# A hybrid decoder step on one core: order from changed prices, weights stored tile by tile, and two rows turned by TensorE

## The chip, the core and the metric

The kernel runs on one core of one Trainium2 chip. The core has five engines that run side by side, each with its own queue of instructions that it works off strictly in order: TensorE (PE in the profile, its weight loads PEld), VectorE (DVE), ScalarE (ACT), GpSimd (POOL) and SyncE (SP), which here only issues DMAs. The metric is the device time of one execution in microseconds (us). An instruction that waits for another engine holds up everything behind it in its own queue, so the order in each queue matters as much as the amount of work.

## The reference

One layer of a decoder for 1024 prompt tokens and 8 single-token samples, all in 32-bit floats, model width 1024:

```python
p = x @ w_in                                    # 1024 x 9360
p_gla, p_rwkv, p_gate = split(p)
# branch 1, gated linear attention, 4 heads, in chunks
#   S_t = diag(a_t) S_{t-1} + k_t^T v_t ;  o_t = q_t S_t
# branch 2, RWKV-7, 16 heads of 64, after a shift by one token
#   S_t = S_{t-1} (diag(w_t) - kk_t^T (kk_t * a_t)) + v_t^T k_t ;  y_t = S_t r_t
m = (sigmoid(gate_a) * (o_gla @ w_up_gla)
     + sigmoid(gate_b) * (o_rwkv @ w_up_rwkv))
y = layernorm(2**0.25 * x + m @ w_out)
```

Each branch norms its output and multiplies it with a gate. The final states of both branches and the last row of the shift are outputs too.

## The kernel before

The tokens are worked in two passes: pass 0 has 512 prompt tokens and the 8 samples (two tiles of 260 columns), pass 1 the other 512 prompt tokens (one tile of 512). Activations lie transposed, features on the 128 partitions. A product with a weight is made in blocks of 128 output features. Weight and input are each split into a high and a low part (`wpart`, `xh`, `xl`), and three products (high with high, high with low, low with high) are summed, 24 matmuls for each tile.

**Weights** (`load_w`). Half a block of a weight, 512 x 128 values, is loaded into a buffer `wraw` of 128 partitions x 512 values (three buffers), ACT rounds it to the high part, DVE subtracts to get the low part, and in pass 0 the split weight is stored to DRAM and loaded from there in pass 1 (`w`). In DRAM `w_in` is a matrix with 9360 columns, so each partition of `wraw` gets four runs of 128 values, 512 bytes each.

**RWKV pairs** (`pair`). Two heads make a pair, 8 pairs in each pass, 16 in all. `front` makes decays and products of a pair: it fills `BK` (a `wide` buffer: 8 chunks of 128 x 128 values, the rows called b and k), `az` and `gg`, sends part of `gg` through DRAM (`LD`) into a second `wide` buffer `L`, and solves a triangular system in 31 steps on DVE (`Xt`, `X`, the first step reads `L`). `back` finishes the inverse. `turn` (lines 1185 to 1204) transposes `BK` and the row v: DVE transposes blocks of 32 x 32, and then copies put each block where it belongs, 16 copies for `BK` and 8 for v in each pair, on ACT or DVE. `chain` runs over the 8 chunks of 64 tokens, one after another, each a row of short steps that go back and forth: a matmul into `pch`, a copy to `rh` on DVE, a matmul, two copies to `u` (a `wide` buffer), a matmul, two DVE operations that make the next state (`Sp` after the last chunk). `norm` ends the pair.

**GLA heads** (`gla_head`) use `row` buffers, a state `S` and PSUM banks called `big`; their transposes are done by TensorE with the identity from `cons`.

**The order** (`Order.run`). Nothing here is ordered by hand. Each strand of work is a generator that offers one operation at a time. A planner keeps a model time for every engine and every tile, prices each operation (`price`), finds when it could start (`start`: when its engine is free and its inputs are ready, plus a margin for the way between engines, `HOP`, and 0.4 us more, `SPARE`, where TensorE reads what another engine made), and takes the one with the earliest start, shifted by a priority. Where an operation may run on two engines (`C`: ACT or DVE, `E`: DVE or POOL), the one that would end it first gets it. The list that comes out is the program; on the chip only that order and the waits on semaphores count. Every recorded operation carries the same line in the profile, L215 (the line in the helper), so its groups are told apart by the names of tiles. Projection matmuls (`proj`) are long in supply and are put between the steps of pairs and heads.

Of the kernel before, what the change touches and what calls it, by code (L numbers as in the profile page):

```python
# [20 lines left out]
P = 128  # L21
D = 1024
NK = D // P
# [3 lines left out]
HT = TP // 2  # L27
# [6 lines left out]
NCH = HT // C  # L34
# [3 lines left out]
OFF_Q, OFF_K, OFF_V, OFF_G, OFF_A = 0, 512, 1024, 2048, 3072  # L38
OFF_R = 3088
# [24 lines left out]
HOP = {"P": 0.2, "D": 0.26, "G": 0.14, "V": 0.14, "A": 0.14}  # L64
# [5 lines left out]
AGE = 0.5  # L70

SPARE = 0.4
BIAS = 0.1
ASIDE = 0.5

# [67 lines left out]
def price(eng, name, out, args, ins):  # L143

    n = out.free_size()
    src = [x for x in ins if x.tensor.space != PSUM] if eng == "A" else ins
    if eng == "P":
        m = args[0].free_size()
        rows, cols = tiles(name, args)
        if name == "transpose":  # L150
            return 0.112
        if args[0].dtype == F32R:
            return max(m / 1200, n / 2200) if rows == cols == P else (m + n) / 1200
        if rows == cols == P:
            return 2 * max(m, n) / 1200 + 0.005
        return 2 * (m + n) / 1200 * rows * cols / P ** 2
    if eng == "S":
        return 0.48
    if eng == "A":
        extra = len(ins) - 1  # L160
        return 0.052 + n / 1200 + (0.042 if len(src) == len(ins) else 0.0) + 0.094 * extra
    wide = max([n, *(x.free_size() for x in ins)]) if name in ("tensor_reduce", "bn_stats", "bn_aggr") else n
    if eng == "V":
        if name == "tensor_tensor_scan":
            return 0.1 + n / 480
        if name in ("tensor_copy", "copy", "memset") and ins and ins[0].tensor.space != PSUM:
            wide = wide / 2
        scalars = sum(x.free_size() == 1 for x in ins[1:]) if name in ("scalar_tensor_tensor", "tensor_scalar") else 0
        return 0.068 + wide / 960 + 0.06 * scalars
    if name in ("tensor_scalar", "memset"):  # L170
        return 0.08 + n / 760
    return 0.1 + n / (300 if name == "tensor_copy" else 456)
# [64 lines left out]
class Order:  # L237
# [83 lines left out]
    def start(self, op):  # L321

        best = None
        for eng, fn, cost in op.ways:
            free, t = self.time[eng] + (SWITCH if eng == "P" and op.tiles != self.tiles else 0.0), 0.0
            for x in (op.out, *op.ins):
                at, by = self.ready.get(x.tensor.name, (0.0, None))
                if eng == "S" and by == "D" and x is op.out:
                    continue
                if by != eng:  # L330
                    at += HOP.get(by, 0.0) + (SPARE if eng == "P" and by in ("V", "A", "G") else 0.0)
                elif eng != "P" and x is not op.out:
                    at += 0.13
                t = max(t, at)
            t = max(t, self.read.get(op.out.tensor.name, 0.0))
            if eng in op.port:
                free = max(free, self.port["G" if eng == "V" else "V"])
            late, t = free - t, max(t, free)
            if eng in "VA" and self.held(eng, op):
                cost += HOLD  # L340
            end = t + cost
            if len(op.ways) > 1:
                end += BIAS if eng == "V" and "A" in op.ways[0][0] else ASIDE if eng == "G" and "G" in op.port else 0.0
            if best is None or end < best[0]:
                best = end, t
                op.eng, op.fn, op.cost, op.late = eng, fn, cost, max(0.0, late)
        return best[1]
# [55 lines left out]
class Kern(Order):  # L403
# [219 lines left out]
    def load_w(self):  # L623

        H = NK // 2
        todo = [(b.src, b.c0, j, b.c.i) for b in self.plan if b.src is not None for j in range(2)]
        raws, his, los, kept = [], [], [], {}

        def high():
            n = 0  # L630
            while True:
                yield lambda: len(raws) > n
                w = yield from self.get("wpart")
                yield self.A.copy(w[:, 0], raws[n][0])
                his.append(w)
                n += 1
                if n == count:
                    return

        def low():  # L640
            for n in range(count):
                yield lambda: len(his) > n
                w = his[n]
                raw, src, c0, j, i = raws[n]
                yield self.E.tensor_sub(w[:, 1], raw, w[:, 0].bitcast(F32))
                self.free(raw)
                los.append(w)
                if src is self.a["w_in"] and i == 0:
                    kept[c0, j] = self.dr.tile([P, 2, 512], F32, name=f"w{c0}_{j}")
                    yield self.S.dma_start(kept[c0, j], w.bitcast(F32))  # L650
                self.ws.append(w)
            self.w_done = True
        count = sum(src is not self.a["w_in"] or i == 0 for src, _, _, i in todo)
        self.spawn(high(), "w")
        self.spawn(low(), "w")
        for n, (src, c0, j, i) in enumerate(todo):
            if src is self.a["w_in"] and i:
                yield lambda: len(los) == len(raws)
                w = yield from self.get("wpart")
                yield self.S.dma_start(w.bitcast(F32), kept[c0, j])  # L660
                self.ws.append(w)
                continue
            raw = yield from self.get("wraw")
            op = self.S.dma_start(raw.rearrange("p (k c) -> p k c", c=P),
                                  src[j * H * P:(j + 1) * H * P, c0:c0 + P].rearrange("(k p) c -> p k c", p=P))
            yield from self.load(f"w{n}", op)
            raws.append((raw, src, c0, j, i))

    def blocks(self):
# [515 lines left out]
    def turn(self, d):  # L1185

        q = [slice(32 * n, 32 * n + 32) for n in range(4)]
        t, tv_ = d.L.rearrange("p (c j f) -> p c j f", c=NCH, j=4), (yield from self.row(HT))
        yield self.V.transpose(d.L, d.BK.rearrange("p c t -> p (c t)"))
        yield self.V.transpose(tv_, d.v[:, :HT])  # L1190
        self.free(d.v)
        for i in range(4):
            for j in range(4):
                yield self.C.copy(d.BK[q[j], :, q[i]], t[q[i], :, j])
        self.free(d.L)
        u = yield from self.get("wide")
        d.u = u.rearrange("p (c h v) -> p c h v", c=NCH, h=2)
        tv = tv_.rearrange("p (c j f) -> p c j f", c=NCH, j=2)
        for h in range(2):
            for i in range(2):  # L1200
                for j in range(2):
                    yield self.C.copy(d.u[q[2 - 2 * h + j], :, h, q[i]], tv[q[2 * h + i], :, j])
        self.free(tv_)
# [445 lines left out]
LANE = ["rwkv_w0", "rwkv_a0", "rwkv_k_k", "rwkv_k_a", "rwkv_r_k", "rwkv_lnx_w", "rwkv_lnx_b"]  # L1649


def layout(i):
    f = np.ascontiguousarray
    cst, lev, heads = constants()
    ch = lambda v: v.reshape(-1, P).T
    pv = np.concatenate([ch(i["rwkv_mu"][0]), ch(i["rwkv_w0"][0]), ch(i["rwkv_a0"][0]), ch(i["rwkv_k_k"][0]),
                         ch(i["rwkv_k_a"][0]), ch(i["rwkv_r_k"][0].reshape(-1)), ch(i["rwkv_lnx_w"][0]),
                         ch(i["rwkv_lnx_b"][0]), ch(i["gla_alpha_b"][0]), ch(i["gla_norm_w"][0])], axis=1)
    xp, xs = i["x_prompt"][0], i["x_sample"][:, 0]
    x = np.concatenate([xp, xs], axis=0)  # L1660
    xT = f(np.concatenate([xp[:HT], xs, xp[HT:]], axis=0).T)
    return {
        "cst": cst, "lev": lev, "heads": heads, "pv": f(pv), "xT": xT, "x": f(x), "w_in": f(i["w_in"][0]),
        "wa": f(i["w_in"][0][:, OFF_A:OFF_R].reshape(NK, P, 16).transpose(1, 0, 2).reshape(P, NK * 16)),
        "gla_alpha_w2": f(i["gla_alpha_w2"][0]), "state_gla": f(i["state_gla"]), "state_rwkv": f(i["state_rwkv"]),
        "shiftT": f(i["state_rwkv_shift"][0].reshape(NS, NRC, P).transpose(2, 1, 0)),
        "lora2": f(np.stack([np.concatenate([i[n][0]] * 2, axis=0) for n in ("rwkv_w2", "rwkv_a2")], axis=1)),
        "lane": f(np.concatenate([i[n][0].reshape(RH, RN) for n in LANE], axis=1)),
        "w_up_gla": f(i["w_up_gla"][0]), "w_up_rwkv": f(i["w_up_rwkv"][0]), "w_out": f(i["w_out"][0]),
        "ln": f(np.concatenate([i["ln_g"], i["ln_b"]], axis=0)),  # L1670
    }

# [19 lines left out]
```

## Time and profile before

| what | value |
|---|---|
| median of 3 runs (lowest to highest) | 1630.72 us (1629.09 to 1632.49) |
| the profiled execution, its time | 1630.17 us |
| its span in the profile | 1628.4 us |
| PE busy, matmuls | 1559.5 us, 96% |
| DVE busy | 1304.1 us, 80% |
| ACT busy | 900.1 us, 55% |
| POOL busy | 131.0 us, 8% |
| DMA, share of 16 engines in use | 62.9% |

The profiled execution took 0.55 us less than the median of the runs; 1.77 us of its time lie outside the span. Busy times of PE come from matmuls that overlap: a matmul's own duration is longer than the distance to the next.

### The profile page before, as it was taken

To read this page: it belongs to the slowest core of one execution; us is meant where nothing else is said; L and a number is where in the kernel's file an instruction comes from. 1 tells how busy PE (TensorE), PEld (TensorE's weight loads), DVE (VectorE), ACT (ScalarE), POOL (GpSimd) and SP (SyncE) were. 2 spreads that over 40 slices of the span, in tenths; PEclk is the share of its full clock that TensorE was granted. 3 is DMA by queue.
4 is the path that set the end of the run, shared out by engine and by line. 5 is a ranking of instruction groups with operands and counts; after the bars stand their busy time and mean duration, and the time that the engine had idled before them with its cause. 6 is when DMAs were issued, how large, how long until landed. Compare 5 with 4: busy or idle time off the path is not lost. (4 is left out here: it accounts for less than half of the span.)

```text
span 1628.4 us, 29162 instructions
## 1 busy us (share of the span) xinstructions
PE 1559.5 (96%) x9874; PEld 1375.1 (84%) x9874; DVE 1304.1 (80%) x3407; ACT 900.1 (55%) x2185; POOL 131.0 (8%) x207
## 2 busy tenths in 40 slices
PE   8999999999999998999999999999899999999998
PEld 7999999998989997787877787787778789977786
DVE  6787899888978897797778898989779877656555
ACT  5557676665677666564755463456344757644210
POOL 1010010000110001000101011111111100000000
PEclk9999999999999999999999999999999999999999
DMA  9867876686767774655555446644563687788432
GB/s 293 261 199 235 250 252 187 207 241 224 235 187 225 247 231 133 218 161 153 155 169 170 123 156 197 177 116 152 159 202 111 197 239 240 232 279 266 143 111 84
DMA packets 287281, 318.27 MB, mean 195 GB/s; under 512 B 87203, under 2 KB 210092, under 8 KB 287132
## 3 DMA queue, kind: packets, MB, share of 16 engines
q1 hardware_dynamic: 287132, 316.40, 62.9%
q8 instruction: 79, 1.29, 0.3%
q14 instruction: 70, 0.57, 0.1%
HBM read 196.66 MB, written 118.61 MB: 194 GB/s over the span
## 5 line engine op out<-in xcount | busy, mean ns | idle before, releaser
L215 PE MATMUL proj<-xh,wpart 128*128 128x260 f32 (+1 forms) x3760 | 927.5, 330 | 1.9 <-DMA wpart<-w 1.1
L215 PEld LDWEIGHTS proj<-xh,wpart 128*128 128x128 f32 x3760 | 630.7, 190 | 52.6 <-issue 5.6
L215 PE MATMUL proj<-xl,wpart 128*128 128x260 f32 (+1 forms) x1880 | 615.5, 327 | 0.0
L215 PEld LDWEIGHTS proj<-xl,wpart 128*128 128x128 f32 x1880 | 356.6, 190 | 25.6 <-issue 3.4
L215 ACT CAST wpart<-wraw 128x512 fp32r<-128x512 f32 x210 | 129.5, 621 | 84.3 <-PE proj L215 37.6
L215 DVE TENSOR_TENSOR row<-row 128x512 f32<-128x512 f32 (+9 forms) x314 | 158.1, 508 | 16.9 <-DMA row<-state_rwkv 9.6
L215 DVE TENSOR_TENSOR wpart<-wraw,wpart 128x512 fp32r<-128x512 f32 x202 | 140.4, 702 | 37.4 <-ACT wpart L215 33.9
L215 ACT ACTIVATE row<-row 128x512 f32<-128x512 f32 (+4 forms) x229 | 138.6, 611 | 33.8 <-DVE row L215 19.4
L215 DVE TENSOR_TENSOR Xt<-X,wide 128x60 f32<-128x60 f32 (+24 forms) x496 | 108.6, 219 | 29.3 <-DMA wide<-LD 18.3
L215 PE MATMUL big<-row 128*128 128x64 f32 (+4 forms) x712 | 116.1, 278 | 8.3 <-DVE S L215 4.2
L215 ACT ACTIVATE s0p<-wide,pc 64x64 f32<-64x64 f32 x256 | 88.2, 344 | 53.1 <-DVE wide L215 40.0
L215 DVE TENSOR_TENSOR X<-X,Xt 128x60 f32<-128x60 f32 (+24 forms) x496 | 108.2, 218 | 10.9
L215 PEld LDWEIGHTS big<-row 128*128 128x128 f32 (+1 forms) x712 | 98.2, 191 | 17.5 <-DVE row L215 4.6
L215 POOL TENSOR_TENSOR row<-row 128x512 f32<-128x512 f32 (+7 forms) x55 | 62.3, 1138 | 560.1 <-DVE X L215 160.0
L215 ACT ACTIVATE row<-proj,omu 128x260 f32<-128x260 f32 (+1 forms) x99 | 54.2, 548 | 92.9 <-PE proj L215 92.3
L215 ACT COPY wide<-pch 64x64 f32<-64x64 f32 x226 | 46.7, 207 | 92.3 <-PE pch L215 85.0
L215 DVE SCALAR_TENSOR_TENSOR wide<-pch,pc,s0p 64x64 f32<-64x64 f32 x224 | 63.0, 281 | 32.0 <-PE pch L215 27.6
L215 ACT COPY wide<-wide 32x256 f32<-32x256 f32 x182 | 73.4, 403 | 23.3 <-DVE wide L215 21.2
L215 ACT COPY row<-big 128x128 f32<-128x128 f32 (+7 forms) x174 | 47.3, 296 | 57.5 <-PE big L215 55.4
L215 DVE SCALAR_TENSOR_TENSOR row<-proj,pv,row 128x259 f32<-128x259 f32 (+1 forms) x99 | 56.3, 569 | 23.7 <-ACT tail L215 14.9
L215 PE MATMUL big<-xh,wpart 128*128 128x260 f32 (+1 forms) x288 | 73.1, 332 | 0.7 <-DVE wpart L215 0.2
L215 PE MATMUL big<-az,wide 128*128 128x256 f32 x256 | 67.5, 395 | 3.8 <-ACT row L215 1.6
(243 smaller groups left out, 2540.5 us busy)
## 6 DMA issues: line engine op xcount, KB each, us to landing
w<-wpart SPq DMA_DIRECT2D x146, 512.0 KB
wpart<-w SPq DMA_DIRECT2D x146, 512.0 KB
wraw<-w_in SPq DMA_DIRECT2D x146, 256.0 KB
wide<-LD SPq DMA_DIRECT2D x64, 128.0 KB
wraw<-w_up_gla SPq DMA_DIRECT2D x32, 256.0 KB
wraw<-w_up_rwkv SPq DMA_DIRECT2D x32, 256.0 KB
sg<-row SPq DMA_DIRECT2D x16, 260.0 KB
row<-sg SPq DMA_DIRECT2D x16, 260.0 KB
```

The lines of the kernel that those rows point to most:

```text
L215: ways.append((eng, lambda call=call: call(out, *args, **kw), price(eng, name, out, args, ins)))
```

## The change

Three things change.

1. **Prices and margins of the planner.** A matmul of 32-bit rounded type costs n/2165 us for n columns, in place of n/2200; issuing a DMA 0.56 us, in place of 0.48; any ACT operation 0.045 us more; and whatever reads a tile that a DMA filled is planned 0.5 us later (`LANDED`).
2. **Weights are laid out on the host** as they are loaded (`blocked`): half a block of `w_in`, `w_up_gla` and `w_up_rwkv` is one contiguous piece, 2 KB for each partition. The load is one plain copy. The number of loads and their bytes stay.
3. **`turn`**: `BK` is transposed by TensorE, four 128 x 128 transposes into one `big` bank and one copy of 128 x 512 back, twice for each pair. The row v goes as before. `u` takes the buffer of `L` in place of another `wide` buffer.

```diff
+LANDED = 0.5
...
-            return max(m / 1200, n / 2200) if rows == cols == P else (m + n) / 1200
+            return max(m / 1200, n / 2165) if rows == cols == P else (m + n) / 1200
...
-        return 0.48
+        return 0.56
...
-        return 0.052 + n / 1200 + (0.042 if len(src) == len(ins) else 0.0) + 0.094 * extra
+        return 0.097 + n / 1200 + (0.042 if len(src) == len(ins) else 0.0) + 0.094 * extra
...
-                    at += HOP.get(by, 0.0) + (SPARE if eng == "P" and by in ("V", "A", "G") else 0.0)
+                    at += HOP.get(by, 0.0) + (SPARE if eng == "P" and by in ("V", "A", "G") else LANDED if by == "D" else 0.0)
...
-            op = self.S.dma_start(raw.rearrange("p (k c) -> p k c", c=P),
-                                  src[j * H * P:(j + 1) * H * P, c0:c0 + P].rearrange("(k p) c -> p k c", p=P))
-            yield from self.load(f"w{n}", op)
+            yield from self.load(f"w{n}", self.S.dma_start(raw, src[c0 // P, j]))
...
     def turn(self, d):
         q = [slice(32 * n, 32 * n + 32) for n in range(4)]
-        t, tv_ = d.L.rearrange("p (c j f) -> p c j f", c=NCH, j=4), (yield from self.row(HT))
-        yield self.V.transpose(d.L, d.BK.rearrange("p c t -> p (c t)"))
+        for x in range(0, NCH, 4):
+            pt = yield from self.bank("big", [P, 4, P])
+            for n in range(4):
+                yield self.tr(pt[:, n], d.BK[:, x + n])
+            yield self.C.copy(d.BK[:, x:x + 4], pt)
+            self.free(pt)
+        tv_ = yield from self.row(HT)
         yield self.V.transpose(tv_, d.v[:, :HT])
         self.free(d.v)
-        for i in range(4):
-            for j in range(4):
-                yield self.C.copy(d.BK[q[j], :, q[i]], t[q[i], :, j])
-        self.free(d.L)
-        u = yield from self.get("wide")
-        d.u = u.rearrange("p (c h v) -> p c h v", c=NCH, h=2)
+        d.u = d.L.rearrange("p (c h v) -> p c h v", c=NCH, h=2)
...
+def blocked(w):
+    return np.ascontiguousarray(w.reshape(2, NK // 2, P, -1, P).transpose(3, 0, 2, 1, 4).reshape(-1, 2, P, NK // 2 * P))
```

With new prices the whole list is dealt anew on every engine. Counted over the program, TensorE gets 128 transposes more (`big<-cons,wide`); DVE loses 16 block transposes of 128 x 1024; 256 block copies (182 on ACT, 74 on DVE) give way to 32 copies of 128 x 512 (26 on ACT, 6 on DVE); of the 256 copies from `pch` to `u`, ACT had 226 and now has 120, DVE had 30 and now has 136; ACT loads its function tables 57 times in place of 49.

DVE at the turn of the fourth pair of pass 0, before (`az`, `wide<-row` and `XT` end `front` and `back`, the copies after the two transposes are `turn`; numbers in names are buffers):

```order
L215 TENSOR_TENSOR az_167<-row 64x8x64 x2
L215 COPY pc<-row 128x8
L215 TENSOR_TENSOR wide<-row 64x8x64 x3
L215 COPY XT_172<-big 32x4x32
L215 TENSOR_TENSOR wide<-row 64x8x64
L215 STREAM_TRANSPOSE wide<-wide 128x1024
L215 STREAM_TRANSPOSE row<-row 128x512
L215 COPY wide<-wide 32x8x32 x15
L215 COPY wide<-row 32x8x32 x8
L215 TENSOR_TENSOR wpart<-wraw,wpart 128x512 x3
L215 COPY rh<-pch 128x128
```

and now, from the first of the two big copies on:

```order
L216 COPY wide<-big 128x512
L216 TENSOR_TENSOR az_167<-row 64x8x64
L216 COPY pc<-row 128x8
L216 TENSOR_TENSOR wide<-row 64x8x64
L216 COPY wide<-big 128x512
L216 STREAM_TRANSPOSE row<-row 128x512
L216 TENSOR_TENSOR wide<-row 64x8x64 x3
L216 COPY wide<-row 32x8x32 x3
L216 TENSOR_TENSOR wpart<-wraw,wpart 128x512
L216 SCALAR_TENSOR_TENSOR row<-row,pv 128x512
```

Twenty-three copies in a row stood between the transposes and the next pair's first `rh`; five remain on DVE, with other work between them.

DVE at the start of the triangular solve of the sixth pair of pass 1, before (`Xt<-X,wide` with 31 columns is the first reader of `L`; `Sp<-pch` makes the last state of the pair ahead):

```order
L215 TENSOR_TENSOR Xt<-X,wide 128x31
L215 TENSOR_TENSOR X<-X,Xt 128x31
L215 TENSOR_TENSOR Xt<-X,wide 128x30
L215 TENSOR_TENSOR X<-X,Xt 128x30
L215 TENSOR_TENSOR Xt<-X,wide 128x29
L215 TENSOR_TENSOR X<-X,Xt 128x29
L215 TENSOR_TENSOR Xt<-X,wide 128x28
L215 TENSOR_TENSOR X<-X,Xt 128x28
L215 TENSOR_TENSOR Xt<-X,wide 128x54
L215 TENSOR_TENSOR X<-X,Xt 128x2x27
L215 SCALAR_TENSOR_TENSOR Sp<-pch,pc,s0p 64x64 x2
L215 TENSOR_TENSOR Xt<-X,wide 128x52
```

and now:

```order
L216 SCALAR_TENSOR_TENSOR Sp<-pch,pc,s0p 64x64 x2
L216 TENSOR_TENSOR row<-st,row 128x512
L216 CAST part<-row 128x512
L216 TENSOR_TENSOR row<-row 128x512
L216 TENSOR_TENSOR part<-row,part 128x512
L216 TENSOR_TENSOR row<-row 128x512 x2
L216 SCALAR_TENSOR_TENSOR row<-big,row 128x512
L216 TENSOR_TENSOR row<-row 128x512
L216 TENSOR_REDUCE row<-row 128x8
L216 TENSOR_TENSOR part<-row,part 128x512
L216 TENSOR_TENSOR Xt<-X,wide 128x31
```

The state now stands ahead of the first reader of `L` with ten other operations between them; before, it stood ten operations behind it.

More of the change, by code (lines that the diff above doesn't have):

```diff
@@ L1662, in layout @@
     return {
-        "cst": cst, "lev": lev, "heads": heads, "pv": f(pv), "xT": xT, "x": f(x), "w_in": f(i["w_in"][0]),
+        "cst": cst, "lev": lev, "heads": heads, "pv": f(pv), "xT": xT, "x": f(x), "w_in": f(np.concatenate([blocked(i["w_in"][0][:, :OFF_A]), blocked(i["w_in"][0][:, OFF_R:])])),
         "wa": f(i["w_in"][0][:, OFF_A:OFF_R].reshape(NK, P, 16).transpose(1, 0, 2).reshape(P, NK * 16)),
@@ L1668, in layout @@
         "lane": f(np.concatenate([i[n][0].reshape(RH, RN) for n in LANE], axis=1)),
-        "w_up_gla": f(i["w_up_gla"][0]), "w_up_rwkv": f(i["w_up_rwkv"][0]), "w_out": f(i["w_out"][0]),
+        "w_up_gla": blocked(i["w_up_gla"][0]), "w_up_rwkv": blocked(i["w_up_rwkv"][0]), "w_out": f(i["w_out"][0]),
         "ln": f(np.concatenate([i["ln_g"], i["ln_b"]], axis=0)),
```

## Prediction

> **What bounds the kernel now.** I read the page's sums first, then the stretches, then who waited for whom, TensorE's waits first.
>
> ```profile
> span 1628.4 us, 29162 instructions
> PE 1559.5 (96%) x9874; PEld 1375.1 (84%) x9874; DVE 1304.1 (80%) x3407; ACT 900.1 (55%) x2185; POOL 131.0 (8%) x207
> PEclk9999999999999999999999999999999999999999
> ```
>
> ```profile
> 1446.23:1451.78 5.55, 5.55 (x26) 4.50 (x25) 2.58 (x4) 2.91 (x5) 0.00 (x0) 1.00 0.76 229
> 100.00:1280.00 1180.00, 1131.70 (x7276) 1004.19 (x7275) 1001.26 (x2772) 704.54 (x1777) 114.15 (x176) 0.99 0.61 188
> 1480.00:1628.40 148.40, 140.65 (x629) 113.90 (x629) 84.51 (x133) 26.67 (x53) 2.77 (x3) 0.99 0.42 133
> ```
>
> TensorE bounds: it is idle for 1628.4 - 1559.5 = 68.9 us, at full clock throughout. 48.3 us of the idle time lie in the long middle (1180 - 1131.7), where projections and pairs are mixed; 7.8 us lie in the last stretch, mostly after its last matmul, and nothing of the change reaches those. So the time is TensorE's own work plus its waits, and an edit is worth what it does to either. Its waits:
>
> ```profile
> PE pch L215 <- DVE wide L215: 8.6, 8, 3.7
> PE big L215 <- DMA row<-xT: 8.0, 5, 4.1
> PE big L215 <- DVE S L215: 7.8, 4, 4.2
> PE big L215 <- DVE part L215: 6.2, 6, 1.4
> PE pch L215 <- DVE rh L215: 6.2, 8, 1.7
> PE big L215 <- DVE Sp L215: 5.7, 2, 4.8
> PE big L215 <- DVE row L215: 4.1, 6, 1.3
> PE proj L215 <- DMA wpart<-w: 1.1, 1, 1.1
> PE proj L215 <- DVE wpart L215: 0.7, 2, 0.4
> ```
>
> The six rows of DVE make 38.6 us; the weights (the last two) make 1.8 us. So TensorE is held up by a DVE that is late, and the question is why it is late. Two places show two causes. At 370 us DVE does the copies of a turn without a break, and the first matmul of a chain waits:
>
> ```profile
> 370.62 4.47 DVE L215 COPY wide<-wide 32x256 f32<-32x256 f32 x15
> 375.11 2.37 DVE L215 COPY wide<-row 32x256 f32<-32x256 f32 x8
> 377.63 0.46 PE L215 MATMUL pch<-wide,gg 128*128 128x128 f32 x2 [3.69 <-DVE wide L215]
> ```
>
> At 1149 us DVE itself waits for a DMA, the one that brings `L`; the state of the chain stands behind that in its queue, and TensorE waits for the state:
>
> ```profile
> 1149.21 0.19 DVE L215 TENSOR_TENSOR Xt<-X,wide 128x31 f32<-128x31 f32 x1 [3.33 <-DMA wide<-LD]
> 1153.42 0.59 DVE L215 SCALAR_TENSOR_TENSOR Sp<-pch,pc,s0p 64x64 f32<-64x64 f32 x2
> 1154.07 0.42 PE L215 MATMUL big<-cons,Sp 128*64 128x128 f32 x1 [4.84 <-DVE Sp L215]
> ```
>
> What DVE waits for, over the whole span:
>
> ```profile
> DVE wpart L215 <- ACT wpart L215: 33.9, 34, 3.8
> DVE row L215 <- ACT row L215: 18.3, 15, 2.5
> DVE Xt L215 <- DMA wide<-LD: 18.3, 11, 4.0
> DVE row L215 <- ACT tail L215: 14.9, 24, 2.4
> DVE row L215 <- DMA row<-state_rwkv: 9.6, 4, 3.3
> DVE S L215 <- ACT row L215: 8.5, 9, 2.4
> ```
>
> For DMAs 27.9 us in 15 waits, 1.86 us each; for ACT 75.6 us in 82 waits, 0.92 us each. These are waits the planner did not foresee, or it would have put other work there.
>
> **The change part by part.** Each term is against the span.
>
> ```profile
> L215 ACT COPY wide<-wide 32x256 f32<-32x256 f32 x182 | 73.4, 403 | 23.3 <-DVE wide L215 21.2
> L215 DVE COPY wide<-wide 32x256 f32<-32x256 f32 x74 | 23.1, 312 | 1.2
> L215 DVE STREAM_TRANSPOSE wide<-wide 128x1024 f32<-128x1024 f32 x16 | 19.8, 1239 | 0.1
> L215 ACT ACTIVATE row<-big,pv 128x512 f32<-128x512 f32 x36 | 23.5, 687 | 8.4 <-PE big L215 8.1
> L215 PE MATMUL big<-cons,row 128*128 128x128 f32 x96 | 16.6, 272 | 0.0
> 625.90 0.49 PE L215 MATMUL big<-cons,row 128*128 128x128 f32 x3
> L215 ACT CAST wpart<-wraw 128x512 fp32r<-128x512 f32 x210 | 129.5, 621 | 84.3 <-PE proj L215 37.6 <-PE big L215 18.3 <-issue 7.0
> ```
>
> *Transposes on TensorE: +14.0.* A transpose takes 272 ns, but three in a row take 0.49 us, so the next ends (0.49 - 0.272)/2 = 0.109 us later; 128 of them make 14.0 us. They lie on the engine that bounds, with nothing to hide them. Ends: 14.0, and 34.8 if none overlapped (128 x 0.272). I take the low end, since the three stand in the same mix of matmuls.
>
> [...]
>
> *The turn's copies: -3.7.* ACT loses 73.4 us, DVE 23.1 + 19.8 = 42.9; 32 copies of 128 x 512 out of PSUM come instead, 32 x 0.687 = 22.0 us by the nearest row, most on ACT. Neither engine bounds, so this counts only where TensorE waited: 3.7 us at 370 us, where the order now leaves five copies. Ends 0 and -8.6, the whole row of `pch` waiting for DVE's `wide`; I take the one wait that is seen behind the copies.
>
> *Margin behind DMAs: -8.3.* `L` hangs on two landings in a row (`LD`, then `L`) and eight issues, so its reader is planned 2 x 0.5 + 8 x 0.08 = 1.64 us later, 88% of a mean wait of 1.86. Of the 38.6 - 3.7 = 34.9 us that are left, DMAs have a share of 27.9 / (27.9 + 75.6) = 27%, so 34.9 x 0.27 x 0.88 = 8.3. The order bears this out at 1149 us, where the state now stands ahead of the reader. Ends 0 and -9.4 (the full share).
>
> *ACT's price: -11.5.* A cast of 128 x 512 was priced 0.052 + 512/1200 + 0.042 = 0.521 us and takes 0.621; the new 0.566 closes 45% of the gap. ACT's share of the 34.9 is 73%: 34.9 x 0.73 x 0.45 = 11.5. Ends -25.5 and, if the new deal makes other waits of the same size, 0.
>
> *Weight loads behind waits: -3.1.* The weight load of a matmul waits too, and part of that does not show as an idle PE:
>
> ```profile
> PEld pch L215 <- DVE rh L215: 16.3, 30, 2.1
> ```
>
> 16.3 us there against 6.2 us of PE: 10.1 us in which the next matmul was not ready while the last still ran. Half of it, 5 us, I count as lost; of DVE's waits (3.7 + 8.3 + 11.5)/38.6 = 61% go, so 3.1. Ends 0 and -6.
>
> *New waits: +4.2.* Each of the 32 groups of transposes needs `BK` finished and a free bank out of three, then a copy; and 106 copies to `u`, 53 steps of chains, move from ACT to the fuller DVE.
>
> ```profile
> L215 ACT COPY wide<-pch 64x64 f32<-64x64 f32 x226 | 46.7, 207 | 92.3 <-PE pch L215 85.0 <-DVE wide L215 2.1 <-issue 1.1
> L215 DVE COPY wide<-pch 64x64 f32<-64x64 f32 x30 | 6.6, 219 | 2.6 <-PE pch L215 1.8 <-issue 0.2
> ```
>
> The copy itself takes as long on either (207 and 219 ns). A chain step that DVE serves costs TensorE 6.2/128 = 0.049 us by the row of `rh` (128 steps); (32 + 53) x 0.049 = 4.2. Ends 0 and 22.0, if every group waited for its copy of 0.687.
>
> *Weights as they are loaded: 0.* 210 loads go from 512 packets of 512 B to 128 of 2 KB.
>
> ```profile
> DMA packets 287281, 318.27 MB, mean 195 GB/s; under 512 B 87203, under 2 KB 210092, under 8 KB 287132
> ```
>
> Packets should fall by 210 x 384 = 80,640 to about 206,600. TensorE waited for weights 1.8 us, so the loads are covered by three raw and four split buffers; were that cover gone, ACT and DVE would show it as waits for `wraw`. Ends -1.8 and 0; a larger packet gives no reason for a loss.
>
> Two edits cost nothing. The first is the matmul's price. The chain of work that ended last has a block of 24 matmuls of 512 columns back to back:
>
> ```profile
> 1446.23 5.55 PE proj L215 x24
> ```
>
> That is 0.231 us each; the old price gave 0.233 and the new gives 0.236, 5 ns apart at most from what is measured, against a margin of 400. The second is eight more table loads on ACT, which is idle for 45% of the span:
>
> ```profile
> L382 ACT ACT_TABLE_LOAD x48 | 61.6, 1283 | 0.8
> ```
>
> 8 x 1.28 = 10.3 us, less than the copies ACT sheds. SP issues the same 1299 DMAs, POOL gets six operations more at 8% busy. What comes late next where DVE's waits go is the chain itself: its steps have about 1 us of projections between them either way.
>
> **The sum.** 14.0 - 3.7 - 8.3 - 11.5 - 3.1 + 4.2 = -8.4, a span of 1620.0. With the 1.77 us outside the span this execution would take 1621.8, and 0.55 more for the median: 1622.
>
> **The rivals.**
>
> *The waits are dealt out anew* (slower). Nothing makes DVE faster: it loses 42.9 us and gets 106 copies (23 us) and 6 big ones (4 us). The margin in front of TensorE stays 0.4 us, and an order dealt anew may hit other late landings as often. Then the margin, ACT's price and the weight loads bring 0 and 14.0 - 3.7 + 4.2 = +14.5 remain: 1645. It decides where those three bring less than 14.5 us together, in place of the 22.9 I count, and the loss is clear below 11.2. For it speaks that DVE is 85% busy in the middle (1001.26 of 1180); against it, that two of the three longest waits are seen to go in the order.
>
> *Transposes do not overlap*, if the data come too late for one to follow the other: 34.8 in place of 14.0, 20.8 more: 1643. Against it stands the row of three. [...]
>
> *The planner becomes right* (much faster). Every wait for DVE goes, with the 5 us of weight loads: 14.0 - 38.6 - 5 + 4.2 = -25.4, 1605. [...] The stretch of those 5.55 us (the first of the three above), in which PE never idles, has 4.50 us of weight loads, 81%, so here 84% is no headroom; the gain ends at the waits.
>
> *It cancels*, recovered waits near 14 us with no new ones: 1631.
>
> **How the numbers follow.** A difference under 0.2%, 3.3 us, cannot be told from none. Forecast, 1613 to 1630: 0.40. Much faster: 0.19. Cancels: 0.07. Waits dealt anew: 0.28. No overlap: 0.06. The forecast's upper end (1627.5 on) counts as the same, about 0.02. Faster is 0.38 + 0.19 = 0.57, same 0.09, slower 0.34. The range runs from 7 us under the much faster case, 1598, for what shortens pipelines beyond idle time, up to the slow rival, 1645; I leave a tenth out on each side.
>
> **What would show it.** Transposes: a group `big<-cons,wide` x128 of about 272 ns, PE's share 97% or more. Turn: no `wide<-wide` on ACT and DVE, 32 `wide<-big`. Margin: `Xt` waiting for `LD` and `row` for the states under 10 us together, from 27.9. ACT's price: DVE waiting for ACT's `wpart` near 20 us, from 33.9. Together: TensorE's six rows of DVE near 19 us, from 38.6. Packets near 206,600. The prediction is wrong if those six rows stay above 30 us, or if the transposes' group has waits of its own above 10 us.

## The result: 0.15% faster, too little to count as a change

| what | before | changed |
|---|---|---|
| median of 20 runs each | 1628.99 us | 1624.84 us |
| lowest to highest | 1620.44 to 1632.49 | 1620.04 to 1631.42 |
| ratio, 95% interval | 1 | 0.9985 [0.9973, 0.9997] |
| profiled execution, its time | 1630.17 us | 1623.65 us |
| PE idle in it (span less busy) | 68.9 us | 49.7 us |

The ratio is worth 2.4 us of 1629, with an interval of 0.5 to 4.4; the medians lie 4.2 us apart, the plain means 3.0. The forecast was a clear gain, 1622.0; the measured time lies 2.8 us above that and inside the range, but the gain by the ratio is under the 0.2% that the prediction itself called no change.

The page's sums of the changed kernel: the span, the engines, the DMA packets.

```profile
span 1621.9 us, 29259 instructions
PE 1572.2 (97%) x10002; PEld 1388.1 (86%) x10002; DVE 1302.8 (80%) x3437; ACT 826.6 (51%) x1917; POOL 133.0 (8%) x213
DMA packets 206641, 318.28 MB, mean 196 GB/s; under 512 B 87203, under 2 KB 102572, under 8 KB 206492
```

PE is 12.7 us busier and 19.2 us less idle. What TensorE waited for (us in total, times, longest), changed kernel:

```profile
PE pch L216 <- DVE rh L216: 5.3, 6, 1.6
PE big L216 <- DMA row<-xT: 5.1, 2, 4.5
PE big L216 <- DVE row L216: 4.6, 10, 0.9
PE big L216 <- ACT row L216: 3.6, 4, 2.1
PE big L216 <- DVE part L216: 3.3, 6, 1.0
PE pch L216 <- DVE wide L216: 2.8, 6, 1.0
PE big L216 <- DVE S L216: 0.3, 1, 0.3
```

The six rows of DVE are down from 38.6 to 16.3 us (`Sp` has no row any more), and none of their waits is longer than 1.6 us; three were 3.7 to 4.8 us. What DVE waited for:

```profile
DVE wpart L216 <- ACT wpart L216: 29.5, 34, 3.5
DVE row L216 <- ACT row L216: 15.1, 14, 2.5
DVE S L216 <- ACT row L216: 15.1, 15, 2.7
DVE row L216 <- ACT tail L216: 11.3, 18, 1.9
DVE Xt L216 <- DMA wide<-LD: 9.5, 9, 1.8
DVE row L216 <- DMA row<-state_rwkv: 1.7, 3, 0.9
```

The two DMA rows fell from 27.9 to 11.2 us. The four rows of ACT fell only from 75.6 to 71.0. The groups that the new `turn` brings:

```profile
L216 PE MATMUL big<-cons,wide 128*128 128x128 f32 x128 | 20.5, 282 | 0.0
L216 ACT COPY wide<-big 128x512 f32<-128x512 f32 x26 | 15.2, 586 | 13.6 <-PE big L216 12.9
L216 DVE COPY wide<-big 128x512 f32<-128x512 f32 x6 | 4.1, 687 | 0.9 <-PE big L216 0.8
```

No transpose made TensorE wait. In this one pair of profiles the totals came out nearly as the sum said, a span 6.5 us shorter for a forecast of 8.4, yet the runs show a third of the forecast gain. Part of the gap is which executions were profiled: that of before took 1.4 us more than the mean of its 20 runs, that of the changed kernel 2.1 us less than its own. The experiments ask how much one pair of orders can tell at all.

### The profile page after: what moved, and what is told of

Its sections match the earlier page's. It is cut to its first block, busy times and chain, and to the rows that moved or that the text cites. A ratio compares the mean times of both kernels' runs of the same rounds, so it can differ in the third digit from the quotient of the medians.

```text
span 1621.9 us, 29259 instructions
## 1 busy us (share of the span) xinstructions
PE 1572.2 (97%) x10002; PEld 1388.1 (86%) x10002; DVE 1302.8 (80%) x3437; ACT 826.6 (51%) x1917; POOL 133.0 (8%) x213
## 5 line engine op out<-in xcount | busy, mean ns | idle before, releaser
L216 PEld LDWEIGHTS proj<-xh,wpart 128*128 128x128 f32 x3760 | 628.1, 189 | 50.5 <-issue 4.3
L216 DVE TENSOR_TENSOR wpart<-wraw,wpart 128x512 fp32r<-128x512 f32 x203 | 141.9, 701 | 31.1 <-ACT wpart L216 29.5
L216 DVE TENSOR_TENSOR row<-row 128x512 f32<-128x512 f32 (+8 forms) x310 | 155.0, 506 | 10.8 <-PE big L216 4.4
L216 DVE TENSOR_TENSOR Xt<-X,wide 128x60 f32<-128x60 f32 (+24 forms) x496 | 109.1, 220 | 20.5 <-DMA wide<-LD 9.5
L216 ACT ACTIVATE s0p<-wide,pc 64x64 f32<-64x64 f32 x256 | 88.2, 344 | 62.6 <-DVE wide L216 50.8
L216 ACT COPY wide<-pch 64x64 f32<-64x64 f32 x120 | 24.8, 206 | 73.9 <-PE pch L216 47.8
```

The lines of the kernel that those rows point to most:

```text
L216: ways.append((eng, lambda call=call: call(out, *args, **kw), price(eng, name, out, args, ins)))
```

## The experiments

Three theories stand against each other. The parts have prices of their own, as the prediction added them up. Or the order dealt anew decides, whatever the parts are worth. Or something that waits do beside leaving TensorE idle is missing from the sum. All ratios are to the kernel before, run beside it on the same chip.

### Each part alone, and the turn taken back

Only `turn` new:

```diff
-        yield self.V.transpose(d.L, d.BK.rearrange("p c t -> p (c t)"))
+        for x in range(0, NCH, 4):
+            pt = yield from self.bank("big", [P, 4, P])
...
```

> Only the turn is changed, prices and weight loads are those of before; the order is dealt anew. Sum of parts (each term of the prediction stands by itself): 14.0 us for the transposes, 4.2 for new waits, 3.7 less for the copies, so about 14.5 us over before, ratio 1.009. Deal by chance (what matters is which waits a new order happens to hit, whatever the edit): within 5 us of before on either side, ratio 0.997 to 1.003, with other places in the list of waits. Clock (a wait of TensorE is followed by a stretch at half clock, so waits cost more than their idle time): the span follows PE's busy time at full clock plus idle time plus half of the stretches at half clock; if the waits fall, ratio under 1.006.

Only the planner's numbers new:

```diff
+LANDED = 0.5
...
-            return max(m / 1200, n / 2200) if rows == cols == P else (m + n) / 1200
+            return max(m / 1200, n / 2165) if rows == cols == P else (m + n) / 1200
...
-        return 0.48
+        return 0.56
...
-        return 0.052 + n / 1200 + ...
+        return 0.097 + n / 1200 + ...
...
```

> Only the planner's prices and the margin behind DMAs are changed, turn and weight loads are those of before. Sum of parts: the margin 8.3, ACT's price 11.5 and the weight loads behind waits 3.1 us less, 22.9 in all, ratio 0.986, and TensorE's waits for DVE near 19 us from 38.6. Deal by chance: ratio 0.997 to 1.003. Clock: the gain is larger than the fall of idle time if the stretches at half clock become fewer, from six (20.4 us) in the trace of before, and smaller if they stay.

The changed kernel with the old `turn`:

```diff
-        for x in range(0, NCH, 4):
-            pt = yield from self.bank("big", [P, 4, P])
...
+        yield self.V.transpose(d.L, d.BK.rearrange("p c t -> p (c t)"))
...
```

> The changed kernel with the turn of before: new prices and weight layout, transposes back on DVE and the copies back on ACT and DVE. Sum of parts: the changed kernel less 14.0 for transposes and 4.2 for new waits, plus 3.7: 14.5 us under it, about 1610, ratio to before 0.989. Deal by chance: within 5 us of the changed kernel, ratio 0.996 to 1.002. If the copies of the turn were what held DVE and ACT up, it is slower than the changed kernel: ratio above 1.000.

| kernel | ratio, 95% interval | PE idle |
|---|---|---|
| turn alone | 1.0035 [1.0017, 1.0053] | 56.4 us |
| planner's numbers alone | 1.0032 [1.0016, 1.0048] | 67.4 us |
| changed, old turn | 1.0078 [1.0056, 1.0101] | 74.0 us |

None of the three is where the sum of parts had it (1.009, 0.986 and 0.989): the planner's numbers, from which the whole gain was hoped, lose 0.3% alone, the turn loses less than its sum, and taking it back loses where it should have gained. For the planner's numbers alone, what TensorE waited for, and then three rows of DVE's waits:

```profile
PE pch L216 <- DVE wide L216: 12.8, 14, 4.8
PE pch L216 <- DVE rh L216: 9.5, 10, 3.6
PE pch L216 <- ACT s0p L216: 4.4, 1, 4.4
PE big L216 <- DVE S L216: 3.4, 5, 1.1
...
DVE wpart L216 <- ACT wpart L216: 33.3, 31, 3.1
DVE Xt L216 <- DMA wide<-LD: 3.0, 3, 1.4
DVE S L216 <- ACT row L216: 2.3, 5, 0.9
```

The margin does what it is for: `Xt` waits 3.0 us for `LD`, from 18.3, and TensorE's waits for `S` and `Sp`, 13.5 us before, are down to 3.4 (`Sp` has no row). But what they gave came back as waits for `wide`, 12.8 us from 8.6, one of 4.8 us at the copies of a turn:

```profile
1092.89 0.80 PE L216 MATMUL pch<-wide,gg 128*128 128x128 f32 x2 [4.84 <-DVE wide L216]
```

So in this order the margin's gain was spent at the old copies. In the changed kernel with the old turn, the row of `wide` is 8.8 us again and the idle time 74.0. It is no rule, though: the planner's numbers with the price of DVE 1 ns higher, a kernel that comes below, keep the old copies and have 1.1 us in that row.

### The weights' layout, with the order held

Kernel before, every instruction in its old place, only the source and the pieces of the weight loads changed (the line with `lag` keeps the planner's idea of the load as it was):

```diff
-            op = self.S.dma_start(raw.rearrange("p (k c) -> p k c", c=P), ...)
+            op = self.S.dma_start(raw, src[c0 // P, j])
+            op.lag = 512 * (0.01 + 512 * 4.65e-5) / 16, 1.7
...
```

> Only the layout of the weights is changed, and the planner keeps the price of the old load, so every engine has the order of before, instruction for instruction. Sum of parts: 0, ratio 0.999 to 1.001, packets 206,641. Rival: packets of 2 KB free the DMA engines, so all landings come earlier, the waits of DVE for LD (18.3 us) and for the states (9.6 us) shrink by a third, and the ratio is 0.996.

And the other way round, the changed kernel in its own order with the old loads:

```diff
-            yield from self.load(f"w{n}", self.S.dma_start(raw, src[c0 // P, j]))
+            op = self.S.dma_start(raw.rearrange("p (k c) -> p k c", c=P), ...)
+            op.lag = 128 * (0.01 + 2048 * 4.65e-5) / 16, 1.7
...
```

> The changed kernel in its own order on every engine, with the weights of before (four runs of 512 bytes for each partition). If the layout's gain of 0.28% in the order of before is the DMAs' own and independent of the order, this is 4.5 us over the changed kernel: ratio to before 1.001 to 1.003, and DVE's waits for LD grow from 9.5 us. If that gain hung on the places where the order of before waits for DMAs, which the new margin has taken away: within 0.001 of the changed kernel.

The layout alone: 0.9972 [0.9959, 0.9984], 1621.29 us. The changed kernel without it: 1.0018 [1.0001, 1.0035]. So it is worth 0.28% in one order and 0.9985 / 1.0018, 0.33% (0.1 to 0.5%), in the other, about 5 us, and without it the change as it stands would be a small loss. In the first of the two orders it is seen where it lies, two rows of DVE's waits:

```profile
DVE Xt L215 <- DMA wide<-LD: 12.1, 11, 2.7
DVE row L215 <- DMA row<-state_rwkv: 8.1, 3, 2.8
```

It is not the weights that come earlier where it counts (TensorE waited for them 1.8 us), but other transfers: with 80,640 packets fewer, `LD` is waited for 12.1 us in place of 18.3, the same 11 times in the same order. That is the third that the rival named; the states' row fell by a sixth. PE idles 61.0 us in place of 68.9.

In the changed kernel's order the waits do not show it. With the old loads the row of `LD` is

```profile
DVE Xt L216 <- DMA wide<-LD: 10.2, 9, 2.0
```

against 9.5 with the new ones, and PE idles 50.8 us against 49.7. The two profiles differ in PE's busy time (1578.3 and 1572.2 us) and in the time at half clock, which is shown below (37.5 and 23.9 us ahead of the end), but over the runs the mean clock is the same (0.991 for both). What the 0.33% is made of in that order stays open.

### The same work in other orders

If order alone moves the time, a price changed by 1 ns, which says nothing new about the chip, must move it too. Three times the kernel before:

```diff
-        return 0.052 + n / 1200 + ...
+        return 0.053 + n / 1200 + ...
```

> The kernel before with one number changed: the planner's price of an ACT operation is 1 ns higher. No operation is added or taken away, but the list is dealt anew on every engine (some 13,000 rows of TensorE's order differ). Deal by chance: the ratio leaves 0.998 to 1.002, as large as the single parts of the change (+0.35, +0.32, -0.28%). Sum of parts, each an effect of its own edit: 1.000 within 0.0015.

```diff
-        return 0.068 + wide / 960 + 0.06 * scalars
+        return 0.069 + wide / 960 + 0.06 * scalars
```

> The same with DVE's price 1 ns higher. Deal by chance: another ratio than the ACT nudge gives, by 0.002 or more from it or from 1. Sum of parts: 1.000 within 0.0015.

```diff
-        return 0.48
+        return 0.481
```

> The kernel before with the price of a DMA issue 1 ns higher. Deal by chance, with the kernel before a lucky one: slower again, ratio 1.003 to 1.009, loss to half clock 25 us. If the ACT and DVE nudges were unlucky and the kernel before is an ordinary deal: ratio 0.995 to 1.002.

They gave 1.0047 [1.0028, 1.0067], 1.0086 [1.0059, 1.0114] and 0.9986 [0.9969, 1.0003]. In this draw one nanosecond on the price of DVE costs 14 us: one wait of 8.1 us and others stand where none stood, as the first row of that kernel's TensorE waits shows.

```profile
PE big L215 <- ACT part L215: 8.9, 2, 8.1
```

An order is thus one draw out of many, and a pair of kernels in different orders compares two draws. The first two of these nudges, and two of other numbers, on the changed kernel (ACT 0.097 to 0.098, DVE 0.068 to 0.069, `HOLD`, a small cost that the planner adds to some operations of ACT and DVE, 0.11 to 0.111, and `SPARE` 0.4 to 0.401):

> The changed kernel with ACT's price 1 ns higher: the same operations, dealt anew. Deals on which the time does not hang (the prices are now right): within 0.002 of the changed kernel. Deal by chance, as in the kernel before: 0.003 to 0.009 slower, with 10 us more lost to half clock. Turn as the carrier (the copies of the old turn make the long waits that halve the clock, so any deal without them loses less): the loss to half clock stays at 13 to 17 us, against 25 to 28 in the nudged deals of before, ratio 0.997 to 1.002.

> The same with DVE's price 1 ns higher. Deal by chance: 0.003 to 0.009 over the changed kernel. Turn as the carrier: loss to half clock 13 to 17 us, ratio 0.997 to 1.002.

> The changed kernel with the planner's hold cost at 0.111 in place of 0.11 us: the work is the same, the list is dealt anew. If the three parts together are worth a gain whatever the deal, and the shipped order is a poor draw of them, this comes out at 0.988 to 0.998 of the kernel before, with TensorE idle 45 to 58 us. If 0.9881 of the deal by the nudged DVE price was luck and the change is worth nothing, 0.998 to 1.006, with TensorE idle 60 us or more or half-clock stretches above 30 us.

> The changed kernel with the margin ahead of TensorE at 0.401 in place of 0.4 us: the same work in another deal. Gain whatever the deal: 0.988 to 0.998 of the kernel before. The change worth nothing: 0.998 to 1.006. With the shipped order and the other three nudges it makes five deals of the changed kernel, whose mean is known to about 0.002 if single deals scatter by 0.4%.

and on the turn alone and the planner's numbers alone:

> The new turn alone, with the prices and weight loads of before and ACT's price 1 ns higher. Carried by the turn: over its deals the turn alone is 0.004 or more under the nudged deals of before (1.0047, 1.0086, 0.9986), so 0.996 to 1.001 here, loss to half clock under 17 us. Carried by the prices: the turn alone stays where it was, 1.002 to 1.007.

> The same with DVE's price 1 ns higher in place of ACT's. Carried by the turn: 0.996 to 1.001. Carried by the prices: 1.002 to 1.007. If a DVE price of 0.069 is itself the better one: under 0.995 here too, as the changed kernel with it (0.9881).

> The new prices alone, with the turn and weight loads of before and ACT's price 1 ns higher still. Carried by the prices: 0.996 to 1.001. Prices of no use while the copies of the old turn stand in the queues: 1.002 to 1.008, with waits of TensorE of 4 us or more for DVE and a loss to half clock of 20 us or more.

> The same with DVE's price 1 ns higher in place of ACT's. Carried by the prices: 0.996 to 1.001. Of no use with the old turn: 1.002 to 1.008, loss to half clock 20 us or more.

| kernel | as it stands | other orders | mean | PE idle, mean |
|---|---|---|---|---|
| before | 1 | 1.0047, 1.0086, 0.9986 | 1.0030 | 70.9 us |
| turn alone | 1.0035 | 1.0041, 1.0081 | 1.0052 | 62.3 us |
| planner's numbers alone | 1.0032 | 1.0041, 0.9952 | 1.0008 | 66.4 us |
| all three parts | 0.9985 | 0.9959, 0.9881, 0.9922, 0.9931 | 0.9936 | 50.5 us |

(The last four intervals of the changed kernel: [0.9944, 0.9973], [0.9858, 0.9904], [0.9904, 0.9940], [0.9908, 0.9954].) Orders of the same work scatter by about 0.4%, 7 us (standard deviation), nearly as much as the whole forecast gain of 8.4. Against that scatter the two families are apart: 0.9936 to 1.0030 is -0.94%, with a 95% interval of -1.6% to -0.27% from the scatter of the nine orders. The nudges of ACT and DVE on the changed kernel came out faster than anything that was expected of them. The last two runs decided it: had 0.9881 been luck and the change worth nothing, they should have come out at 0.998 or above; both lie well below. So over orders the change is worth some 0.9%, and the pair at hand shows little of it because the old order was a good draw of its kind (1 against 1.0030) and the new one the worst of five (0.9985 against 0.9936). Two of these orders compute wrong outputs, with relative errors up to 0.34 and 0.49: before with DVE's nudge (1.0086), and the planner's numbers with ACT's (1.0041). Why is not known, nor whether the fault moved their times. Without them the mean of before is 1.0011 and the difference -0.75%, with an interval of -1.4% to -0.1%; the mean of the planner's numbers is 0.9992. The gain is smaller then, but stays.

The page of the best, the changed kernel with DVE's price at 0.069, 1606.41 us, 0.9881 [0.9858, 0.9904], which beats both:

```profile
span 1604.7 us, 29235 instructions
PE 1558.3 (97%) x10002; PEld 1383.6 (86%) x10002; DVE 1304.9 (81%) x3434; ACT 831.4 (52%) x1930; POOL 131.4 (8%) x205
```

Neither the turn nor the planner's numbers lie clearly under 1 alone (means 1.0052 and 1.0008). It may be that the two need each other, but the layout brings 0.3% by itself, and with three orders each a mean is known to 0.0025 only. The nudged orders of the turn stayed above 1, those of the planner's numbers went one each way, so it isn't settled. That 0.069 is simply a better price of DVE is out: with it the turn alone has 1.0081 and the kernel before 1.0086.

### What the transposes cost

The changed kernel in its own order, each of the 128 transposes issued twice:

```diff
-                yield self.tr(pt[:, n], d.BK[:, x + n])
+                op = self.tr(pt[:, n], d.BK[:, x + n])
+                op.ways = [(e, lambda f=f: (f(), f()), c) for e, f, c in op.ways]
+                yield op
```

> The changed kernel in its own order, with each of the 128 transposes on TensorE issued twice (the second overwrites the first with the same values). TensorE bounds: 128 x 0.109 = 14.0 us over the changed kernel's 1624.8, ratio to before about 1.007 to 1.008. Not overlapping (0.272 each): 34.8 us, ratio 1.020. Hidden in waits that stand there anyway: under 4 us, ratio 0.999 to 1.001.

1.0028 [1.0008, 1.0047]; against the changed kernel 1.0028 / 0.9985, +0.43%, 7.0 us. The page's sums:

```profile
span 1627.7 us, 29515 instructions
PE 1581.4 (97%) x10130; PEld 1402.1 (86%) x10130; DVE 1302.9 (80%) x3437; ACT 827.5 (51%) x1917; POOL 132.7 (8%) x213
```

The group of transposes in the same kernel:

```profile
L216 PE MATMUL big<-cons,wide 128*128 128x128 f32 x256 | 34.4, 277 | 0.0
```

That lies between two of the expectations, 14.0 us and under 4, and far from 34.8; with the intervals of the two ratios it is 3 to 11 us. 128 more add 9.2 us to PE's busy time and 7.0 us to the run: 0.055 to 0.072 us each. The 277 ns of a transpose are a duration and not a cost. The group's own busy time grew by 13.9 us (20.5 to 34.4), 0.109 each, just the distance that the prediction used; a part was made up elsewhere, by less idle time (49.7 to 46.3 us) and 3.4 us less at half clock (20.5 us in place of 23.9, see below).

### Waits and the clock

The traces showed something that the prediction had missed when it read "at full clock throughout" from the page's line of tenths: behind long waits the granted clock of TensorE was 0.50, here for 3.41 and 30.72 us. The stretches around the wait of 4.84 us at 1149 us in the kernel before, and around a longer one, 14.3 us, in the turn alone with the nudged DVE price (us, then busy us of PE, PEld, DVE, ACT and POOL, then the granted clock, the DMA share and GB/s):

```profile
1150.40:1153.81 3.41, 0.00 (x0) 0.00 (x0) 3.17 (x9) 0.00 (x0) 2.32 (x3) 1.00 0.27 109
1153.81:1157.22 3.41, 3.15 (x8) 2.54 (x9) 2.96 (x11) 1.00 (x3) 1.02 (x2) 0.50 0.04 5
1157.22:1160.63 3.41, 3.41 (x16) 2.75 (x15) 3.06 (x13) 0.00 (x0) 0.00 (x0) 1.00 0.50 159
```

```profile
1295.00:1298.23 3.23, 0.36 (x3) 0.02 (x1) 2.96 (x12) 2.37 (x5) 0.00 (x0) 1.00 1.08 370
1298.23:1328.95 30.72, 9.53 (x40) 8.71 (x41) 19.45 (x60) 10.08 (x19) 0.00 (x0) 0.50 0.43 120
1328.95:1340.00 11.05, 11.05 (x95) 11.05 (x95) 4.15 (x10) 7.28 (x18) 0.00 (x0) 1.00 0.36 104
```

In the first, 8 matmuls fall into the 3.41 us at a clock of 0.50 and 16 into the next 3.41 us, at 1.00. To see whether idle time is the cause, the changed kernel with the old turn (54.6 us at half clock ahead of its end) got 59 extra matmuls with the identity, put ahead of three matmuls that end long waits:

```diff
+    def warmed(self, op, out, n):
...
+            def first(f):
+                for _ in range(n):
+                    self.nc.tensor.matmul(out, self.ident, w, start=True, stop=True)
+                f()
...
```

> The kernel with the turn undone in its own order, with matmuls on constants put ahead of three waits of TensorE (5.2, 4.8 and 4.2 us, at 613, 1376 and 1127 us), into the bank that the waiting matmul fills next: 22, 20 and 17 of them, 4.8, 4.4 and 3.7 us by 0.218 each. The waits stay, TensorE is busy in them. Clock: the three stretches at half clock behind them (17.1, 13.7 and 6.8 us) go, half of their 37.6 us is won: 18.8 us under the turn undone, ratio to before 0.996 to 0.998, granted clock 0.994 from 0.983. If idle time does not set the clock: the same clock, ratio 1.008 or somewhat more.

1.0109 [1.0080, 1.0138] against 1.0078 without. The gain of 18.8 us did not come. The stretches at half clock shrank from 54.6 to 41.0 us in all, the three that were aimed at from 37.6 to 20.5 (none of them went, but behind the two waits that were filled they begin 6 and 13 us later), and the mean granted clock over the runs rose from 0.9833 to 0.9865. Of the three sets the one at 1127 us ran after its wait and not in it: TensorE still idled 3.1 us ahead of it. The extra matmuls cost 10 us of work for some 5 us of clock: where two waits were filled, the stretches behind them began later and got shorter, so idle time bears on the clock in this kernel, and filling it doesn't pay here.

Over all runs a kernel's time can be split by the mean granted clock, as an estimate: the span times one minus the clock is what the half clock took, the rest is about what the program would take at full clock. (TensorE also waits inside some stretches, so the first is an upper bound: of the 30.72 us above it was busy for 9.53.) Means of the four orders of before and the five of the changed kernel:

| | at full clock | lost to the clock |
|---|---|---|
| before, four orders | 1609.1 us | 20.8 us (13 to 28) |
| all three parts, five orders | 1603.8 us | 11.2 us (7 to 15) |
| difference | -5.3 us | -9.6 us |

By this split two thirds of what the change is worth is clock, though neither share is known closely: the intervals are -17 to -2 us for the clock and -12 to +1 for the rest, and without the order of before that computes wrong outputs the clock's share is -7.2. And here the pair at hand is unlucky on both sides: the old order lost 13 us, the least of its four; the new one 14.9, the most of its five.

## Why the prediction was right and wrong

On the page the totals of the sum nearly hold. PE's busy time rose by 12.7 us, where the terms had 14.0 - 3.1 = 10.9, and its idle time fell by 19.2, where they had 3.7 + 8.3 + 11.5 - 4.2 = 19.3. What failed are steps behind those totals, one term put at nothing, and the reading of one order as the price of the edit.

- **Transposes: +14.0.** The overlap was right and the rival *Transposes do not overlap* is out: 128 more cost 7.0 us, not 34.8. As a size the term is between 7 and 14: the distance of 0.109 us was right, but not all of it reaches the span, and the doubled ones lie back to back, which the first ones need not.
- **The turn's copies: -3.7.** Right in place in this pair: the row of `pch` waiting for `wide` fell by 5.8 us (8.6 to 2.8). As a price it is not shown: over the orders that row goes from 2.5 to 8.6 us before and from 1.7 to 9.4 in the changed kernel.
- **Margin behind DMAs: -8.3.** The mechanism is shown: the two DMA rows fell to 11.2 us where under 10 were named, and over the orders they have 12.0 to 27.9 us before, 3.0 to 8.8 with the planner's numbers alone and 8.0 to 12.2 in the changed kernel. What it saves TensorE is not: no run has the margin apart from the prices, and the planner's numbers by themselves left 67.4 us idle, over three orders 66.4 against 70.9.
- **ACT's price: -11.5.** This is the step that failed. It took 45% off DVE's waits for ACT; they fell from 75.6 to 71.0, 6%, and the row of `wpart`, named at 20 us, stood at 29.5. Over the orders the four rows have a mean of 79.0 us before, 62.2 with the planner's numbers alone and 69.6 in the changed kernel, so the fall is 12 to 21%, under half of what was counted; `wpart` never came under 25.7. By the term's own formula, 34.9 x 0.73 x the fall, that is 1.5 us in this pair and 3.1 to 5.3 over the orders, in place of 11.5. That TensorE's six rows still came out where the text said, 16.3 for 19, is a match of totals and not of causes: those rows alone have 24.1 to 38.6 us over the orders of before, and this old order is the highest.
- **Weights as they are loaded: 0.** Failed, and outside its ends (-1.8 to 0): -0.28% and -0.33%, about 5 us, in two orders. The packets were right to 41. The step asked who waits for the weights; in the order of before the gain lies with those who wait for other transfers, whose rows were on the page at 27.9 us.
- **New waits: +4.2.** None seen at the transposes, and the row of `rh` fell from 6.2 to 5.3 us; too large.
- **Weight loads behind waits: -3.1.** The row that it rests on fell less than the text had it:

```profile
PEld pch L216 <- DVE rh L216: 13.3, 25, 2.0
```

Less the 5.3 us of PE that is 8.0 us, from 10.1. Half of the difference, as the term counts it, is 1.0; the half itself was not tested.
- **Missing:** a price for the half clock. The trace of before has 20.5 us at a granted clock of 0.5 ahead of its end, which a line of tenths does not show; up to 10 us lie there between the families of orders.
- **The rivals.** *The waits are dealt out anew*, the slower one, is right in its mechanism, and for either part alone it also had the sign. For all three together it holds for a draw and not for the mean. *The planner becomes right* is out, since 16.3 of the 38.6 us stand. *It cancels* comes nearest to the measured ratio, but its reason, recovered waits near 14 us, is not what the page shows.

The failure of the text as a whole is that it gave one order's time to a few microseconds, and 0.09 to "same", where an edit of 1 ns scatters the time by 7 us.

With ACT's term at 1.5 the sum is +1.6 in place of -8.4, and with the 5 us of the layout about -3, next to the 2.4 measured. That is no proof: with the transposes at 7 us and no new waits, as the bullets also have it, it would be about -15, the difference of the means over orders, and far from this pair. So the runs show which terms were mis-sized, and not that the corrected sum is right.

## What to carry to other kernels

Where a planner deals the order, nudge a price by 1 ns a few times before and after an edit and compare the means; one pair of orders says little about an edit worth less than 1%, and the best draw may be kept (here 0.9881), if its outputs are right: two of the orders here compute wrong ones. Hold the order and change one physical thing, as with the loads, when its own price is wanted. When packets fall, look at who waits for any DMA, and where a trace shows the clock halved behind waits of TensorE, as here behind all six of 2.1 us and longer in the two profiles of before and changed, price such a wait above its idle time.

## What the runs showed that was not expected

**Behind TensorE's six longest waits the granted clock was 0.50.** In the kernel before, six stretches run at a granted clock of 0.50 ahead of the end, each 3.41 us long, at 379, 543, 632, 935, 1154 and 1185 us; in the changed kernel four, 10.2 us at 610, 6.8 at 692, 3.4 at 1020 and 1184. In these two profiles PE stood idle between matmuls for 2.1 us or longer in one piece six times (3.69, 4.17, 2.58 and 4.84 us in before, 2.10 and 2.63 in the changed kernel), and each time such a stretch began, five times 0.5 to 1.4 us after the idle time and once, at 1154 us, 0.3 us ahead of its end. Below that it isn't sharp: of 25 idle times of 1.01 to 1.72 us four had a stretch within 2.6 us behind them (1.15 us twice in before, 1.64 and 1.13 in the changed kernel), and 21 had none (up to 1.72 us). What sets these four apart was not shown.

**Much of the spread of the runs goes with the clock.** Of the 20 runs of the changed kernel the slowest took 1631.42 us at a mean clock of 0.987, the fastest 1620.04 at 0.994 (correlation -0.89). In the other kernels with ten runs or more it is -0.46 to -0.90, and in one, the layout alone, there is none (0.05). Why the clock differs between runs of one program was not shown.
